# Half a chunk of weights ahead of x, and four pool maps in three products of two parts

## The chip, the core and the metric

The kernel runs on one core of one Trainium2 chip. The metric is the device time of one execution in microseconds (us), the median of several runs. The engines are named as in the profile: PE multiplies matrices (PEld is its loading of stationary operands), DVE and ACT work elementwise on vectors, POOL does the same and indirect transfers, and SP only issues transfers. The queues of SP, ACT and POOL share 16 DMA engines.

## What is computed

A decoder layer on 512 tokens of 1024 features in fp32. A mixing sublayer comes first, then a mixture of 32 experts (top 4), then a gated embedding; each ends in a layer norm. The change lies in the mixing sublayer, and there in the pooling mixer:

```python
proj = x @ w_in[i]                    # (512, 1024) @ (1024, 2048)
v_pool = proj[..., :D_POOL]           # four groups of 128 channels
...
y_pool = pool_mixer(v_pool, pool_mix[i], pool_scale[i])
y_conv = conv_mixer(b_gate, c_gate, v_conv, conv_w[i])
mix = jnp.concatenate([y_pool, y_conv], axis=-1) @ w_out[i]
...
# pool_mixer: group g has the trailing window w = 2, 4, 8, 16
outs.append((cs - lagged) / cnt - vg)                 # the pool difference d
y = jnp.einsum('bsgc,gcd->bsgd', d, pool_mix)         # the map: 128 x 128 for each group
return y.reshape(B, S, D_POOL) * pool_scale
```

## The kernel before

**Two parts.** The large products are made from two parts of each operand: a high part rounded to the format that the listing calls F32R (`nc.scalar.copy`, on ACT), and the low part, the difference (`nc.vector.tensor_sub`, on DVE). `mm3` (line 210) issues three products for each pair of operands: high with low, high with high, low with high. They are lines 213, 214 and 215 in the profile, whatever calls them.

**Weights.** All weights pass through a ring of buffers of 1 MB in chunks, in a fixed order: `load` (line 96) issues the next chunk on SP's queue, `split` (line 105) makes its two parts, `done` gives the buffers back and starts the loads that now have room. The first chunk of the input projection is loaded in two halves of 512 KB, 128 columns each (`c_in[0]`); the other seven hold 256 columns.

**The start.** x comes in four blocks of 128 tokens. SP's queue holds block 0, the first half chunk, block 1, the second half chunk, blocks 2 and 3, and then the other chunks. `turned(i)` transposes block i on PE in two halves of four (line 315, into PSUM tiles `tr`, of which there are two), and for each half ACT writes the high part `xh` (line 394) and DVE the low part `xl` (line 395). `keep_warm` (line 204) issues products whose results nobody reads; `WARM_START` says how many stand before block 0, before block 1 and after it. Then `columns` runs the first half chunks on the first 256 tokens, with blocks 2 and 3 turned between.

**The projection.** The loop at line 486 goes through the chunks in the order 0, 1, 4, 6, 2, 5, 7, 3; a chunk of 256 columns takes 48 products of 512 columns. The program's order is written out by hand, and every engine runs its instructions in that order:

```python
for f in (pool_diff, pool_map):
    for m in pools:
        f(m)
```

Chunks 0 and 1 hold the pool groups (1 and 0, then 3 and 2). After a chunk, `pool_sums` copies its columns out of PSUM and makes the trailing sums on DVE or POOL. One chunk later, behind that chunk's 48 products, `pool_diff` (lines 448 to 451, DVE) makes the difference d, and `pool_map` (line 460) maps it: one product in fp32, 128x512 (line 463; PE runs it as two passes, two records of the profile), a scaled copy on ACT (line 464), and `mixed` (line 454), which writes the two parts of the mixed tokens into the tiles `y`: four casts on ACT (line 457) and four subtractions on DVE (line 458), one for each block of tokens. `y` is read again by the output projection, `project`, after the loop. `bsp` is a tile that `bias_parts` fills during the output projection.

Of the kernel before, what the change touches and what calls it, by code (L numbers as in the profile page):

```python
# [10 lines left out]
F32 = mybir.dt.float32  # L11
F32R = mybir.dt.float32r
# [8 lines left out]
P = 128  # L21
S = 512
NT = S // P
D = 1024
# [12 lines left out]
SPARE = 1  # L37
RING = 14

WARM_START, WARM_ROUTE, WARM_END = (6, 7, 7), (2, 2, 2), (8, 3)  # L40
TURN1 = 5
EMBED = 18
MAXOV = 32
# [5 lines left out]
def tile_layer(ctx: ExitStack, tc: tile.TileContext, x, p, w_in, pool_mix, pool_scale, conv_w, w_out,  # L49
               ln1_g, ln1_b, router_w, router_b, w_gate_up, b_gate_up, w_down, b_down,  # L50
               ln2_g, ln2_b, ple_proj, ple_gate_w, ple_gate_b, ln3_g, ln3_b, out):
    nc = tc.nc
# [8 lines left out]
    def at(name, b, dtype, n=2048, offset=0):  # L61

        return nc.alloc_sbuf_tensor_at(name, [P, n], dtype, offset=base0 + 8192 * b + 4 * offset).ap()
# [6 lines left out]
    def big(n=P):  # L70
        return ps.tile([n, 2, 512], F32, tag="big", name="big", bufs=3)
# [15 lines left out]
    def take(dtype, *kinds):  # L87

        b = next(k for k in kinds if k).popleft()
        return (b[0].tile([P, 2048], dtype, tag=b[1], name="chunk") if type(b) is tuple else ring[b][dtype == F32R]), b  # L90
# [5 lines left out]
    def load(queue=nc.sync, *kinds):  # L96
        j = nloaded[0]
        src, shape = chunks[j]
        t, b = take(F32, *(kinds or (free,)))
        t = t[:, :shape[0] * shape[1]].rearrange("p (a b) -> p a b", a=shape[0])  # L100
        raws[j] = t, b
        queue.dma_start(t, src)
        nloaded[0] += 1
# [26 lines left out]
    def splittable():  # L130
        n, two = room(nsplit[0])
        moved = type(raws[nsplit[0]][1]) is tuple
        return n > moved and two >= moved
# [24 lines left out]
    def splits(n=E):  # L158
        while n and nsplit[0] < min(limit[0], used[0] + lookahead[0]):
            if nloaded[0] == nsplit[0]:  # L160
                load()
            if not splittable():
                break
            split()
            n -= 1
            fill()
# [37 lines left out]
    def keep_warm(n, a, b, o=None):  # L204

        o = big()[:, 0, :b.shape[-1]] if o is None else o
        for _ in range(n):
            nc.tensor.matmul(o, a, b, start=True, stop=True)  # L208

    def mm3(o, ah, al, bh, bl, start, stop, a_late=False):  # L210

        first, last = ((ah, bl), (al, bh)) if a_late else ((al, bh), (ah, bl))
        nc.tensor.matmul(o, *first, start=start, stop=False)  # L213
        nc.tensor.matmul(o, ah, bh, start=False, stop=False)  # L214
        nc.tensor.matmul(o, *last, start=False, stop=stop)  # L215
# [44 lines left out]
    bsp = cp.tile([P, F], F32R, name="bsp")  # L260
# [106 lines left out]

    pro = tc.alloc_tile_pool(name="pro", bufs=1)

    y = [at(f"y{i}", RING + i, F32R) if i < NT - 1 else pro.tile([P, 2 * D], F32R, name="y") for i in range(NT)]  # L370
    y = [[t[:, k * D:(k + 1) * D].rearrange("p (c t) -> p c t", c=ND) for k in range(2)] for t in y]
    with tc.tile_pool(name="mix", bufs=1, side=RIGHT) as q:
        cols16 = q.tile([16, P], F32, name="cols16")
        pmix = q.tile([P, 4, P], F32, name="pmix")
# [3 lines left out]
        xl = q.tile([P, ND, S], F32R, name="xl")  # L378
        with tc.tile_pool(name="xin", bufs=1, side=RIGHT) as xp:
            xs = [xp.tile([P, D], F32, tag="xs", name="xs", bufs=NT) for _ in range(NT)]  # L380
            for i in range(NT):
                nc.sync.dma_start(xs[i], x[0, i * P:(i + 1) * P, :])
                if i < 2:
                    load()
            load()
            nc.sync.dma_start(cols16[:12], conv_w[0].rearrange("k (j p) -> (k j) p", p=P))
            nc.sync.dma_start(cols16[12:16], pool_scale[0].rearrange("(j p) -> j p", p=P))
            nc.sync.dma_start(pmix, pool_mix[0].rearrange("g c d -> c g d"))
            fill()

            def turned(i):
                def put(h, t):
                    o = (slice(None), slice(4 * h, 4 * h + 4), slice(i * P, (i + 1) * P))
                    nc.scalar.copy(xh[o], t)
                    nc.vector.tensor_sub(xl[o], t, xh[o].bitcast(F32))
                transposed(xs[i], P, put)

            def columns(o, cs, b, ts_, between={}):

                wh, wl = (parts[cs[b]] if len(cs) == 2 else (q[:, :, b * P:(b + 1) * P] for q in parts[cs[0]]))  # L400
                for k in range(ND):
                    if k in between:
                        turned(between[k])
                    mm3(o[:, b, ts_], wh[:, k], wl[:, k], xh[:, k, ts_], xl[:, k, ts_], k == 0, k == ND - 1,
                        a_late=True)

            keep_warm(WARM_START[0], ident, ident)
            turned(0)
            splits(1)
            keep_warm(WARM_START[1], ident, ident)  # L410
            turned(1)
            keep_warm(WARM_START[2], ident, ident)
            splits(1)
            o1 = big()
            columns(o1, c_in[0], 0, slice(0, 256), {4: 2})
            columns(o1, c_in[0], 1, slice(0, 256), {2: 3})
            for b in range(2):
                columns(o1, c_in[0], b, slice(256, S))
            splits()
# [2 lines left out]
        cols = q.tile([P, 16], F32, name="cols")  # L422
        nc.vector.tensor_copy(cols, tcol)
        wp = tc.alloc_tile_pool(name="wide", bufs=1, side=RIGHT)

        def wide(tag):
            return wp.tile([P, 16 + S], F32, tag=tag, name=tag, bufs=4)

        held = {}
# [24 lines left out]
        def mixed(c, v):  # L454
            for i, (yh, yl) in enumerate(y):
                ts_ = slice(i * P, (i + 1) * P)
                nc.scalar.copy(yh[:, c], v[:, ts_])
                nc.vector.tensor_sub(yl[:, c], v[:, ts_], yh[:, c].bitcast(F32))

        def pool_map(g):  # L460
            t = tr([P, S])
            d = held.pop(("d", g))
            nc.tensor.matmul(t, pmix[:, g], d, start=True, stop=True)
            nc.scalar.activation(d, t, AF.Copy, scale=cols[:, 12 + g:13 + g])
            mixed(g, d)

# [15 lines left out]
            nc.vector.tensor_mul(v, o, v)  # L482
            mixed(4 + m, v)

        pools = []
        for j, cs in zip(order_in, c_in):
            o = o1 if len(cs) == 2 else big()
            for b in range(2):
                if len(cs) == 1:
                    columns(o, cs, b, slice(0, S))  # L490
            for f in (pool_diff, pool_map):
                for m in pools:
                    f(m)
            pools = []
            for b in (1, 0):
                kind, m = divmod(2 * j + b, 4)
                (pool_sums, conv_out, conv_gate, conv)[kind](m, o[:, b])
                if kind == 0:
                    pools.append(m)
            for c in cs:  # L500
                parts.pop(c)
                done(c)
            splits()
# [401 lines left out]
    for e in range(E):  # L905
# [3 lines left out]
        for o, n, c in halves:  # L909
            r, s = slice(c // 16, c // 16 + 32), slice(e // 16 * 512, e // 16 * 512 + 512)  # L910
            nc.tensor.matmul(o[:, n], sel[r, e % 16:e % 16 + 1].to_broadcast([32, CAP]), bsp[r, s],
                             start=True, stop=False)
# [226 lines left out]
```

## Time and profile before

| | |
|---|---|
| median of 3 runs | 1401.81 us (1401.22 to 1402.82) |
| the profiled execution | 1401.93 us |
| its span, first to last instruction | 1400.1 us |
| mean granted clock of PE | 0.996 |
| PE busy | 1378.5 us, 98% |
| DVE busy | 1225.1 us, 88% |
| ACT busy | 948.1 us, 68% |
| POOL busy | 480.8 us, 34% |
| read from memory | 443.97 MB, 331 GB/s over the span |

An engine's busy time counts its own work, not its waits. A record of a product lasts longer than the pace at which products follow one another, because they are pipelined; costs on PE are therefore read from the starts of records. A line of a timeline gives start, duration, engine, line of the program, operation, written tile and read tiles, shapes, how many records are merged, and in brackets the idle time before the first of them and what ended it. Line numbers are those of the kernel before.

### The profile page before, as it was taken

The page shows a single profiled execution, that of the slowest core. Times are in us where ns is not written, and L with a number is a line of the kernel's source. Part 1 is how long each engine was busy: PE and PEld are TensorE (multiplying, and loading weights), DVE is VectorE, ACT ScalarE, POOL GpSimd, SP SyncE. Part 2 cuts the span into 40 slices and gives each one's busy share as a digit, 9 for nine tenths or more (in the row PEclk, how much of TensorE's full clock was granted, in tenths as well). Part 3 has the DMA queues.
Part 4 walks back from the last instruction along what each step waited for, and adds up shares of the span by engine and source line. Part 5 has one row for each costly group of instructions (what it writes and reads, how often), then busy time and mean ns, then how long its engine had stood idle before and what let it go on. Part 6 is the DMA issues. An engine that isn't in the chain of part 4 may idle for free. (4 is left out here: it accounts for less than half of the span.)

```text
span 1400.1 us, 17688 instructions
## 1 busy us (share of the span) xinstructions
PE 1378.5 (98%) x6605; PEld 987.5 (71%) x6605; DVE 1225.1 (88%) x1078; ACT 948.1 (68%) x740; POOL 480.8 (34%) x171
## 2 busy tenths in 40 slices
PE   9999999999999999999999999999999999999996
PEld 8788767766677777676777667666666666666675
DVE  6645599999999999999989999999999999999875
ACT  5321267777777777777777778777777777777631
POOL 1101114533333333333333363545454545442100
PEclk9999999999999999999999999999999999999999
DMA  9327889999999999999989999999999999999511
GB/s 330 129 90 241 331 315 367 370 376 386 375 380 380 378 369 385 384 374 381 323 318 335 376 381 396 371 394 391 385 357 386 381 385 367 365 388 363 172 47 46
DMA packets 98264, 464.44 MB, mean 332 GB/s; under 512 B 9488, under 2 KB 19232, under 8 KB 65408
## 3 DMA queue, kind: packets, MB, share of 16 engines
q1 hardware_dynamic: 86640, 427.85, 78.9%
q0 software_dynamic: 9536, 33.44, 9.6%
q10 hardware_dynamic: 2000, 1.98, 0.5%
q8 instruction: 54, 0.88, 0.3%
q14 instruction: 34, 0.28, 0.1%
HBM read 443.97 MB, written 19.27 MB: 331 GB/s over the span
## 5 line engine op out<-in xcount | busy, mean ns | idle before, releaser
L321 POOL DMA_INDIRECT xg<-x1d,idxg x31 | 227.9, 7350 | 254.9 <-ACT chunk L114 109.4
L361 POOL DMA_INDIRECT acc<-yo,idxs x32 | 179.7, 5615 | 39.3 <-ACT yo L360 23.8
L213 PE MATMUL big<-chunk,xl 128*96 128x512 f32 x480 | 190.3, 396 | 0.0
L214 PE MATMUL big<-chunk,xh 128*96 128x512 f32 x480 | 189.0, 394 | 0.0
L346 POOL TENSOR_SCALAR h<-h 96x1024 f32<-96x1024 f32 x32 | 41.0, 1280 | 401.5 <-ACT h L345 401.5
L213 PE MATMUL big<-chunk,hl 128*96 128x512 f32 x268 | 106.4, 397 | 0.0
L214 PE MATMUL big<-chunk,hh 128*96 128x512 f32 x268 | 104.9, 391 | 0.0
L213 PEld LDWEIGHTS big<-chunk,xl 128*96 128x96 f32 x480 | 77.4, 161 | 34.9 <-issue 3.4
L214 PEld LDWEIGHTS big<-chunk,xh 128*96 128x96 f32 x480 | 77.4, 161 | 30.8
L214 PEld LDWEIGHTS big<-chunk,hh 128*96 128x96 f32 x268 | 43.7, 163 | 17.5
L213 PEld LDWEIGHTS big<-chunk,hl 128*96 128x96 f32 x268 | 43.1, 161 | 17.1
L349 ACT ACTIVATE sg<-gm 96x1024 f32<-96x1024 f32 x32 | 34.0, 1064 | 16.2 <-DVE gm L343 16.2
L330 ACT CAST xh<-tr 128x384 fp32r<-128x384 f32 x64 | 27.4, 480 | 25.4 <-PE tr L315 25.4
L360 ACT ACTIVATE yo<-big,gs 96x1024 f32<-96x1024 f32 x31 | 34.4, 1111 | 13.4 <-PE big L215 13.4
L299 POOL TENSOR_TENSOR mv<-mv,mhalf 128x1 f32<-128x1 f32 x12 | 7.8, 653 | 97.2 <-DVE mv L298 97.2
L330 ACT CAST hh<-tr 128x384 fp32r<-128x384 f32 x62 | 26.5, 479 | 20.3 <-PE tr L315 20.3
L353 DVE SCALAR_TENSOR_TENSOR h<-h,gm 96x1024 f32<-96x1024 f32 x32 | 38.9, 1215 | 0.2
L351 DVE TENSOR_TENSOR gm<-gm,sg 96x1024 f32<-96x1024 f32 x32 | 38.9, 1215 | 0.1
L343 DVE TENSOR_SCALAR gm<-big 96x1024 f32<-96x1024 f32 x32 | 38.7, 1210 | 0.0
L117 DVE TENSOR_TENSOR ring12dt.float32r<-ring12dt.float,ring6dt.float32r 128x2048 fp32r<-128x2048 f32 x14 | 32.0, 2287 | 4.9 <-ACT ring6dt.float32r L114 4.9
L345 ACT COPY h<-big 96x1024 f32<-96x1024 f32 x32 | 32.6, 1020 | 5.4 <-PE big L215 5.4
L117 DVE TENSOR_TENSOR ring9dt.float32r<-ring9dt.float,ring2dt.float32r 128x2048 fp32r<-128x2048 f32 x14 | 32.0, 2288 | 4.0 <-ACT ring2dt.float32r L114 4.0
(583 smaller groups left out, 4397.6 us busy)
## 6 DMA issues: line engine op xcount, KB each, us to landing
ring13dt.float<-in_w_gate_up_dram SPq DMA_DIRECT2D x18, 1024.0 KB, 9.2
ring10dt.float<-in_w_gate_up_dram SPq DMA_DIRECT2D x18, 1024.0 KB, 7.8
ring1dt.float<-in_w_gate_up_dram SPq DMA_DIRECT2D x18, 1024.0 KB, 8.5
ring2dt.float<-in_w_gate_up_dram SPq DMA_DIRECT2D x18, 1024.0 KB, 8.4
ring3dt.float<-in_w_gate_up_dram SPq DMA_DIRECT2D x18, 1024.0 KB, 8.5
ring4dt.float<-in_w_gate_up_dram SPq DMA_DIRECT2D x18, 1024.0 KB, 9.5
ring9dt.float<-in_w_gate_up_dram SPq DMA_DIRECT2D x17, 1024.0 KB, 9.2
ring5dt.float<-in_w_gate_up_dram SPq DMA_DIRECT2D x17, 1024.0 KB, 7.3
```

The lines of the kernel that those rows point to most:

```text
L117: second()
L213: nc.tensor.matmul(o, *first, start=start, stop=False)
L214: nc.tensor.matmul(o, ah, bh, start=False, stop=False)
L321: nc.gpsimd.indirect_dma_start(out=xg, out_offset=None, in_=x1d, in_offset=bass.IndirectOffsetOnAxis(ap=idxg[:, e:e + 1], axis=0))
L330: nc.scalar.copy(hi[:, 4 * h:4 * h + 4], t)
L343: nc.vector.tensor_scalar(gm, gp, LIMIT, None, op0=ALU.min)
L346: nc.gpsimd.tensor_scalar(h, h, LIMIT, -LIMIT, op0=ALU.min, op1=ALU.max)
L349: nc.scalar.activation(sg, gm, AF.Sigmoid, scale=SW_ALPHA)
L351: nc.vector.tensor_mul(gm, gm, sg)
L353: nc.vector.scalar_tensor_tensor(h, h, 1.0, gm, op0=ALU.add, op1=ALU.mult)
L360: nc.scalar.activation(y, o.rearrange("p a b -> p (a b)"), AF.Copy, scale=gate)
L361: nc.gpsimd.indirect_dma_start(out=acc, out_offset=bass.IndirectOffsetOnAxis(ap=idx, axis=0), in_=y, in_offset=None, compute_op=ALU.add)
```

## The change

The first half chunk of weights is loaded ahead of x, and the second behind block 1. At the start the split of the first half chunk is issued ahead of block 0, that of the second right behind block 1, and the warm-up calls are 13, 2 and 3. The map weights `pmix` are split into two parts `mh` and `ml`, which lie in `bsp`. Behind the chunk in which `pool_map` stood, `pool_parts` now writes the two parts of d to the places in `y` where the group's mixed tokens will stand; one chunk later `pool_map` makes the map from the parts with `mm3`, in 384 columns (the three blocks that now lie in one tile, `y012`) and 128 (the last block), and `mixed` overwrites the places.

```diff
--- before.py
+++ after.py
@@ -37,7 +37,7 @@
 SPARE = 1
 RING = 14
 
-WARM_START, WARM_ROUTE, WARM_END = (6, 7, 7), (2, 2, 2), (8, 3)
+WARM_START, WARM_ROUTE, WARM_END = (13, 2, 3), (2, 2, 2), (8, 3)
 TURN1 = 5
 EMBED = 18
 MAXOV = 32
@@ -367,7 +367,8 @@
 
     pro = tc.alloc_tile_pool(name="pro", bufs=1)
 
-    y = [at(f"y{i}", RING + i, F32R) if i < NT - 1 else pro.tile([P, 2 * D], F32R, name="y") for i in range(NT)]
+    y012 = at("y012", RING, F32R, (NT - 1) * 2048).rearrange("p (i q) -> p i q", i=NT - 1)
+    y = [y012[:, i] if i < NT - 1 else pro.tile([P, 2 * D], F32R, name="y") for i in range(NT)]
     y = [[t[:, k * D:(k + 1) * D].rearrange("p (c t) -> p c t", c=ND) for k in range(2)] for t in y]
     with tc.tile_pool(name="mix", bufs=1, side=RIGHT) as q:
         cols16 = q.tile([16, P], F32, name="cols16")
@@ -378,9 +379,10 @@
         xl = q.tile([P, ND, S], F32R, name="xl")
         with tc.tile_pool(name="xin", bufs=1, side=RIGHT) as xp:
             xs = [xp.tile([P, D], F32, tag="xs", name="xs", bufs=NT) for _ in range(NT)]
+            load()
             for i in range(NT):
                 nc.sync.dma_start(xs[i], x[0, i * P:(i + 1) * P, :])
-                if i < 2:
+                if i == 1:
                     load()
             load()
             nc.sync.dma_start(cols16[:12], conv_w[0].rearrange("k (j p) -> (k j) p", p=P))
@@ -404,13 +406,13 @@
                     mm3(o[:, b, ts_], wh[:, k], wl[:, k], xh[:, k, ts_], xl[:, k, ts_], k == 0, k == ND - 1,
                         a_late=True)
 
+            splits(1)
             keep_warm(WARM_START[0], ident, ident)
             turned(0)
-            splits(1)
             keep_warm(WARM_START[1], ident, ident)
             turned(1)
+            splits(1)
             keep_warm(WARM_START[2], ident, ident)
-            splits(1)
             o1 = big()
             columns(o1, c_in[0], 0, slice(0, 256), {4: 2})
             columns(o1, c_in[0], 1, slice(0, 256), {2: 3})
@@ -423,6 +425,10 @@
         nc.vector.tensor_copy(cols, tcol)
         wp = tc.alloc_tile_pool(name="wide", bufs=1, side=RIGHT)
 
+        mh, ml = (bsp[:, k * 512:(k + 1) * 512].rearrange("p (g d) -> p g d", g=4) for k in range(2))
+        nc.scalar.copy(mh, pmix)
+        nc.vector.tensor_sub(ml, pmix, mh.bitcast(F32))
+
         def wide(tag):
             return wp.tile([P, 16 + S], F32, tag=tag, name=tag, bufs=4)
 
@@ -457,10 +463,17 @@
                 nc.scalar.copy(yh[:, c], v[:, ts_])
                 nc.vector.tensor_sub(yl[:, c], v[:, ts_], yh[:, c].bitcast(F32))
 
+        def pool_parts(g):
+
+            mixed(g, held["d", g])
+
         def pool_map(g):
             t = tr([P, S])
             d = held.pop(("d", g))
-            nc.tensor.matmul(t, pmix[:, g], d, start=True, stop=True)
+
+            dh, dl = (y012[:, :, k * D + g * P:k * D + (g + 1) * P] for k in range(2))
+            mm3(t[:, :S - P].rearrange("p (i t) -> p i t", t=P), mh[:, g], ml[:, g], dh, dl, True, True)
+            mm3(t[:, S - P:], mh[:, g], ml[:, g], y[-1][0][:, g], y[-1][1][:, g], True, True)
             nc.scalar.activation(d, t, AF.Copy, scale=cols[:, 12 + g:13 + g])
             mixed(g, d)
 
@@ -482,16 +495,18 @@
             nc.vector.tensor_mul(v, o, v)
             mixed(4 + m, v)
 
-        pools = []
+        pools, ready = [], []
         for j, cs in zip(order_in, c_in):
             o = o1 if len(cs) == 2 else big()
             for b in range(2):
                 if len(cs) == 1:
                     columns(o, cs, b, slice(0, S))
-            for f in (pool_diff, pool_map):
+            for m in ready:
+                pool_map(m)
+            for f in (pool_diff, pool_parts):
                 for m in pools:
                     f(m)
-            pools = []
+            pools, ready = [], pools
             for b in (1, 0):
                 kind, m = divmod(2 * j + b, 4)
                 (pool_sums, conv_out, conv_gate, conv)[kind](m, o[:, b])
```

PE at the start of the program (`big<-ident` are the warm-up calls, `tr<-ident,xs` the transposes of a block, `big<-xl` and `big<-xh` the first products of the projection):

```order
-L208 MATMUL big<-ident 128x128 x6
+L208 MATMUL big<-ident 128x128 x13
 L315 MATMUL tr<-ident,xs 128x128 x8
-L208 MATMUL big<-ident 128x128 x7
+L208 MATMUL big<-ident 128x128 x2
 L315 MATMUL tr<-ident,xs 128x128 x8
-L208 MATMUL big<-ident 128x128 x7
+L208 MATMUL big<-ident 128x128 x3
 L213 MATMUL big<-xl,ring9dt.float32r 128x256
```

Most of the warm-up calls now stand ahead of block 0, and three are left between block 1 and the first product.

ACT in the same place (`xh<-tr` are the high parts of x, `ring9dt` and `ring10dt` those of the two half chunks); DVE has the low parts in the same order:

```order
-L394 CAST xh<-tr 128x4x128 x2
 L114 CAST ring9dt.float32r<-ring0dt.float_63 128x1024
-L394 CAST xh<-tr 128x4x128 x2
+L396 CAST xh<-tr 128x4x128 x4
 L114 CAST ring10dt.float32r<-ring1dt.float_65 128x1024
-L394 CAST xh<-tr 128x4x128 x4
+L396 CAST xh<-tr 128x4x128 x4
 L114 CAST ring11dt.float32r<-ring2dt.float_67 128x2048
```

The first half chunk's part moved ahead of block 0, and blocks 0 and 1 now follow one another.

PE behind the third chunk of the projection (`ring12dt` and `ring3dt` are that chunk's parts; `tr<-v,pmix` are maps as before, `tr<-y,bsp` maps from parts):

```order
 L215 MATMUL big<-xh,ring3dt.float32r 128x512
-L463 MATMUL tr<-v,pmix 128x512 x2
+L213 MATMUL tr<-y_160,bsp 128x384
+L214 MATMUL tr<-y_160,bsp 128x384
+L215 MATMUL tr<-y_160,bsp 128x384
+L213 MATMUL tr<-y,bsp 128x128
+L214 MATMUL tr<-y,bsp 128x128
+L215 MATMUL tr<-y,bsp 128x128
```

Where the maps of groups 3 and 2 stood, the maps of groups 1 and 0 now stand, the second of them in six products like these; the maps of groups 3 and 2 follow behind the fourth chunk.

## Rows read from the trace of the kernel before

**Rows 1.** The page, busy time of the engines.

```profile
PE 1378.5 (98%) x6605; PEld 987.5 (71%) x6605; DVE 1225.1 (88%) x1078; ACT 948.1 (68%) x740; POOL 480.8 (34%) x171
```

**Rows 2.** Busy time by stretch: us, engines busy (instructions), PEclk, DMA share, GB/s.

```profile
35.00:110.00 75.00, 74.47 (x312) 58.22 (x313) 40.97 (x70) 23.60 (x48) 8.03 (x15) 1.00 0.32 113
...
170.00:1000.00 830.00, 827.64 (x3952) 577.93 (x3953) 776.76 (x601) 627.83 (x448) 331.24 (x80) 1.00 0.98 370
```

**Rows 3.** Waits of the matmul engine, whole span: total us, times, longest.

```profile
PE tr L648 <- DVE xl L331: 0.8, 1, 0.8
PE tr L315 <- DMA xs<-in_x_dram: 0.7, 2, 0.5
```

**Rows 4.** Timeline of PE, 1 to 10.6 us: start, us, engine, line, operation, tiles.

```profile
1.38 2.93 PE L208 MATMUL big<-ident 128*128 128x128 f32 x12 [1.38 <-DVE ident L225]
4.54 1.09 PE L315 MATMUL tr<-ident,xs 128*128 128x128 f32 x8 [0.22 <-DMA xs<-in_x_dram]
...
7.72 1.07 PE L315 MATMUL tr<-ident,xs 128*128 128x128 f32 x8 [0.52 <-DMA xs<-in_x_dram]
...
10.10 0.36 PE L213 MATMUL big<-xl,ring9dt.float32r 128*128 128x256 f32 x1
```

**Rows 5.** Warm-up products by form, 0 to 4.4 and 5.4 to 7.3 us: busy, mean ns.

```profile
L208 PE MATMUL big<-ident 128*128 128x128 f32 x12 | 2.9, 434 | 1.4 <-DVE ident L225 1.4
...
L208 PE MATMUL big<-ident 128*128 128x128 f32 x14 | 1.7, 275 | 0.0
```

**Rows 6.** Timeline of the SP queue, then DMA issues (KB each, us from issue to landing).

```profile
1.17 0.42 SPq L102 DMA_DIRECT2D ring0dt.float<-in_w_in_dram  x1
...
ring0dt.float<-in_w_in_dram SPq DMA_DIRECT2D x1, 512.0 KB, 5.0
```

**Rows 7.** Timelines of ACT and DVE, 5 to 13 us.

```profile
6.24 1.06 ACT L114 CAST ring9dt.float32r<-ring0dt.float 128x1024 fp32r<-128x1024 f32 x1
...
5.90 1.29 DVE L395 TENSOR_TENSOR xl<-tr,xh 128x512 fp32r<-128x512 f32 x2 [2.51 <-ACT xh L394]
7.33 1.22 DVE L117 TENSOR_TENSOR ring0dt.float32r<-ring0dt.float,ring9dt.float32r 128x1024 fp32r<-128x1024 f32 x1
9.00 1.29 DVE L395 TENSOR_TENSOR xl<-tr,xh 128x512 fp32r<-128x512 f32 x2 [0.45 <-ACT xh L394]
```

**Rows 8.** Timeline of PE around the four maps.

```profile
33.30 0.39 PE L213 MATMUL big<-xl,ring11dt.float32r 128*128 128x512 f32 x1
...
34.47 0.40 PE L215 MATMUL big<-xh,ring2dt.float32r 128*128 128x512 f32 x1
35.20 2.00 PE L463 MATMUL tr<-v,pmix 128*128 128x512 f32 x4 [0.34 <-issue]
...
37.27 0.39 PE L214 MATMUL big<-xh,ring12dt.float32r 128*128 128x512 f32 x1
...
48.01 0.40 PE L215 MATMUL big<-xh,ring3dt.float32r 128*128 128x512 f32 x1
48.73 1.97 PE L463 MATMUL tr<-v,pmix 128*128 128x512 f32 x4 [0.33 <-DVE v L451]
...
50.77 0.40 PE L214 MATMUL big<-xh,ring13dt.float32r 128*128 128x512 f32 x1
```

**Rows 9.** Timeline of PE, products of 256 columns; eight more lie between these.

```profile
10.42 0.28 PE L215 MATMUL big<-xh,ring0dt.float32r 128*128 128x256 f32 x1
...
11.47 0.28 PE L215 MATMUL big<-xh,ring0dt.float32r 128*128 128x256 f32 x1
```

**Rows 10.** Timeline of DVE, 34 to 50 us.

```profile
34.94 0.16 DVE L451 TENSOR_TENSOR v<-s,v 128x3 f32<-128x3 f32 x1
...
38.91 0.90 DVE L458 TENSOR_TENSOR y<-v,y 128x128 fp32r<-128x128 f32 x4 [0.62 <-ACT y L457]
...
46.78 1.51 DVE L448 SCALAR_TENSOR_TENSOR v<-s,v 128x497 f32<-128x497 f32 x1
...
49.29 0.17 DVE L451 TENSOR_TENSOR v<-s,v 128x7 f32<-128x7 f32 x1
```

## The prediction, made before the change was run

> **What bounds the kernel now.** I read the page first, then the stretches, then the waits, then the timelines of the first 50 us. The matrix engine (PE) is busy 98% of the span [rows 1], and in the two long stretches, the input projection from 35 to 110 us and the experts from 170 to 1000 us, it is busy 74.5 of 75.0 and 827.6 of 830.0 us [rows 2]. Its waits are few: the only row that names a transfer is the arrival of x at the very start, 0.7 us in two waits, and the longest wait inside the expert stage is 0.8 us, for DVE [rows 3]. So the end is set by the sum of what PE executes plus its few gaps. A microsecond taken from PE at the start should come off the end, because what follows (expert loads, splits, gathers) is released by PE's own products; a microsecond added to ACT or DVE there costs nothing while they have room: in 35 to 110 us DVE is busy 41 us and ACT 23.6 us of 75 [rows 2]. The change touches only the first 60 us, at two places: the start of the projection, and the four pool maps.
>
> **The start.** Before, x's first block is first in the queue and the first weights second. PE starts on x's first block at 4.54, right on its arrival, and the weights land at 1.17 + 5.0 = 6.17 [rows 4, 6]. Now the weights go first (0.42 us of issue on SP [rows 6]), so block 0 of x takes the second place. Both are 512 KB from one queue, so I take 6.2 for its transposes, 1.65 later. What follows by the old distances: the first half of a turned block leaves its PSUM buffer when DVE has its low part, 5.90 + 0.65 = 6.55, which is 2.0 after PE began, and the second half at 7.19, 2.65 after [rows 4, 7]. There are two such buffers, so block 1, whose x was there at 7.72 [rows 4], can begin at 6.2 + 2.0 = 8.2 instead. From its beginning to DVE's work on its low part it took 9.00 - 7.72 = 1.28 [rows 4, 7], and the half takes 0.65: the first projection product can run at 8.2 + 1.28 + 0.65 = 10.15 or a little over, say 10.2. Before it ran at 10.10 [rows 4], though its data was complete at 9.65: the seven warm-up calls ahead of it kept PE. So the old start was set by filler, the new one by data, and the difference is **+0.1 us**. What was won, that the weights' split (1.06 on ACT, 1.22 on DVE [rows 7]) is no longer between the two blocks, goes into waiting for x. The bounds: -0.4 (it starts when the data was complete before) and +1.05 (rival three).
>
> The warm-up calls move with this: 6, 7, 7 become 13, 2, 3, two records to a call. The first twelve records ran at (2.9 - 0.43)/11 = 0.22 us each, fourteen later ones at (1.7 - 0.275)/13 = 0.11 [rows 5], the ratio of the two clock levels, 1.2 and 2.4 GHz (read off the durations; the granted clock of the page shows no such stretch). Twenty-six records then end near 1.38 + 12 x 0.22 + 14 x 0.11 = 5.6, ahead of 6.2; the four and the six end before the data they lead to. They cost nothing; with x early, those left over would cost 0.11 each.
>
> **The pool maps.** Before, each pair of maps stands behind a chunk's 48 products and needs pool differences that DVE finishes only then: 34.94 + 0.16 = 35.10, and PE's map starts at 35.20 [rows 8, 10]. The products before come every (34.47 - 33.30)/5 = 0.234 us [rows 8]. From the last one before a pair to the second one after it PE took 37.27 - 34.47 = 2.80 and 50.77 - 48.01 = 2.76, where two paces are 0.47 [rows 8]. The pairs cost **2.33 and 2.29, together 4.62 us**; some 0.5 of each is the wait (35.20 against 34.47 + 0.23 = 34.70), the rest, 1.84, four passes of 512 columns at 0.46.
>
> Now a pair is two times three products of 384 columns and three of 128, in the format of the projection. 384 columns by its pace: 0.75 x 0.234 = 0.176. A product of 128 columns in this format stands nowhere in the trace. Lower bound: half of the 256-column pace, (11.47 - 10.42)/9 = 0.117 [rows 9], so 0.058. Upper bound: as the old format, a quarter of two passes of 0.46, so 0.23. I take 0.115: every record here brings its own load of 128 weight columns, and the shortest records that do, the 128-column warm-up passes, follow at 0.11 [rows 5], no faster than the 256-column products with twice the columns. A pair is then 6 x 0.176 + 6 x 0.115 = 1.75, two pairs 3.50: **-1.12 us**; with the bounds 0.058 and 0.23, -1.8 and +0.25. The Trainium skill bears on this against the split into a long and a short piece: "TensorE: Matmul & The Clock Gate", section LDWEIGHTS, says a load's time goes with the weights' columns alone, some 107 ns for 128, so that a short product would not outrun its load; by that figure the pairs would come to 3.40 and the time, as an estimate, to 1400.7. No run here shows it for this format.
>
> Is the wait really gone? The first pair's parts are now cast and subtracted one chunk before PE wants them. DVE's differences are pushed back by the new split of the maps, 128x512, about 0.7, and the parts follow; before, even with the maps in between, they were done at 38.91 + 0.90 = 39.8 [rows 10], and PE wants them at 48.01 + 0.23 [rows 8], less the 2.33 of the pair that is gone, plus 0.1: 46.0: seven us of room. The second pair is tighter, since its differences now queue on DVE behind the first pair's mixing, which waits for PE's maps. That mixing ended 39.8 - 35.2 = 4.6 after the maps began, so 50.6; the differences take 49.46 - 46.78 = 2.7 [rows 10], the parts 1.3 more, since ACT and DVE share them: 54.6. PE wants them at 46.0 + 1.75 + 48 x 0.234 = 59.0. Room of 4.4 us. The extra parts, four groups of four casts and four subtractions (0.90 us a group on DVE [rows 10], on ACT the like), are 3.6 us on each, under idle time. If that cover went, PE would wait at the second pair first.
>
> **Sum.** +0.1 - 1.12 = -1.0 us. The profiled execution took 1401.93 (span 1400.1, 1.8 around it) and becomes 1400.9; it lay 0.1 above the median of 1401.81, so I predict **1400.8**. Differences under 0.2%, 2.8 us, I call no change, and this is one.
>
> **Rivals.**
> One: the short products run at the old format's rate, 0.23. For it: 128 columns are few and nothing in the trace shows this format so narrow. Against it: 256 columns still run at the full pace. The pairs become 4.87, the sum +0.35: 1402.2.
>
> Two: their loads hide wholly, 0.058: the pairs 2.81, the sum -1.7: 1400.1. Against it stand the 0.11 of [rows 5]. The Trainium skill, same page, section on the back-to-back issue gap, has a stream of 128-column products with their loads at some 81 ns; by that the pairs would be 3.08 and the time, as an estimate, 1400.4; the nearest rows here are slower.
>
> Three, slower: the first weights and block 0 of x share the transfer engines and both land at 6.2. ACT and DVE work in order, and the weights' split now stands ahead of block 0, so 1.06 + 1.22 [rows 7] comes first: x's first half has its low part at 9.15 and the projection starts at 9.15 + 1.28 + 0.65 = 11.1, 1.05 late. PE would stand still in between; if the granted clock then fell to 1.2 GHz for as long as at the beginning, twelve records at 0.22 instead of 0.11 show the price, 1.3 to 1.4 more. Sum 1.05 + 1.35 - 1.12 = +1.3: 1403.1, more if the fall lasts. It decides from a landing of the weights after 5.2 (DVE must be through by 7.55). Against it: block 0 of x, first in the queue and as large, was there by 4.54, 1.6 ahead of the second.
>
> Four: the gain doesn't reach the end, because the experts' transfers, busy 98% at 370 GB/s [rows 2], set the pace: 1401.8. Against it: PE is busy 827.6 of 830 there and no wait names a transfer.
>
> **Numbers.** My forecast 0.55, rival one 0.17, two 0.10, three 0.10, four 0.08. Range 1399.0 to 1403.2: from the sum of the lower bounds, -1.8 - 0.4, less the half spread of the runs shown (0.6), up to rival three. Under 1399.0 I put a third of rival two and a tenth of my own case: 0.08. Over 1404.6 half of rival three and a little of one: 0.07. The rest, 0.85, is no measurable change.
>
> **What would show it.** In the new profile: PE's first projection product at 10.2 (over 11: rival three); the six plus six products between two chunks taking 1.75 us, the 128-column ones 0.115 apart (0.23: rival one; 0.06: rival two); no wait of PE on DVE there; PE's first expert product 1 us earlier, and the end too (if only the first: rival four). A gap ahead of the second pair would show my room of 4.4 us wrong, and a gap in the experts that was not there before would make the whole sum wrong.

## The result: 8.4 us slower, and the profile after

| | before | changed |
|---|---|---|
| median | 1400.68 us (6 runs, 1399.79 to 1402.82) | 1409.09 us (6 runs, 1407.48 to 1411.30) |
| profiled execution, its span | 1401.93, 1400.1 | 1408.78, 1407.0 |
| mean granted clock | 0.996 | 0.994 |

The ratio on record is 1.0057, with a 95% interval from 1.0046 to 1.0068 (it is estimated from all the runs and need not be the quotient of the two medians): slower by more than 0.2%, and outside the predicted range. The two profiled executions differ by 6.85 us; the medians differ by 1.6 more, most likely from how executions of one kernel fall (a part on this stands behind the experiments). One of the 20 runs of the kernel before that serve experiment 7 took 3514 us and is left out of the ratios there.

The waits of PE after the change, the first two rows (total us, times, longest), have a transfer at their head, which stood nowhere in [rows 3]:

```profile
PE big L213 <- DMA ring15dt.float<-in_w_gate_up_dram: 5.6, 1, 5.6
PE big L1043 <- issue: 2.2, 1, 2.2
```

The timeline of PE after the change (start, duration, the idle time before in brackets): the start, the first pair of maps, and the output projection from the last product of block 1 to the router's first product (L592, which is L577 before). The blocks are the four blocks of tokens; block 0 is the first, and the third is the one in the third part of `y`.

```profile
1.38 4.62 PE L208 MATMUL big<-ident 128*128 128x128 f32 x26 [1.38 <-DVE ident L225]
6.19 1.09 PE L315 MATMUL tr<-ident,xs 128*128 128x128 f32 x8 [0.20 <-DMA xs<-in_x_dram]
...
8.30 1.25 PE L315 MATMUL tr<-ident,xs 128*128 128x128 f32 x8 [0.57 <-DVE xl L397]
...
10.45 0.36 PE L213 MATMUL big<-xl,ring9dt.float32r 128*128 128x256 f32 x1 [0.23 <-DVE xl L397]
...
46.04 0.40 PE L215 MATMUL big<-xh,ring3dt.float32r 128*128 128x512 f32 x1
46.27 0.34 PE L213 MATMUL tr<-y,bsp 128*128 128x384 f32 x1
...
46.80 0.22 PE L213 MATMUL tr<-y,bsp 128*128 128x128 f32 x1
46.85 0.27 PE L214 MATMUL tr<-y,bsp 128*128 128x128 f32 x1
46.97 0.27 PE L215 MATMUL tr<-y,bsp 128*128 128x128 f32 x1
47.08 0.39 PE L213 MATMUL tr<-y,bsp 128*128 128x384 f32 x1
47.31 0.34 PE L214 MATMUL tr<-y,bsp 128*128 128x384 f32 x1
...
48.23 0.39 PE L214 MATMUL big<-xh,ring13dt.float32r 128*128 128x512 f32 x1
...
127.25 0.39 PE L215 MATMUL big<-ring12dt.float32r,y 128*128 128x512 f32 x1
133.21 0.80 PE L213 MATMUL big<-ring4dt.float32r,y 128*128 128x512 f32 x1 [5.57 <-DMA ring15dt.float<-in_w_gate_up_dram]
133.81 0.63 PE L214 MATMUL big<-ring4dt.float32r,y 128*128 128x512 f32 x1
...
139.80 1.93 PE L592 MATMUL tr<-early,rw 128*32 128x128 f32 x16
```

The same two places in the output projection before, and two in the last 80 us, of which more below (timeline of PE before the change):

```profile
128.10 0.39 PE L215 MATMUL big<-ring12dt.float32r,y 128*128 128x512 f32 x1
128.32 0.39 PE L213 MATMUL big<-ring4dt.float32r,y 128*128 128x512 f32 x1
...
132.72 1.93 PE L577 MATMUL tr<-early,rw 128*32 128x128 f32 x16
...
1324.19 0.73 PE L1028 MATMUL big<-bd,gt 96*128 96x512 f32 x2 [2.37 <-issue]
...
1330.37 0.50 PE L213 MATMUL big<-ring4dt.float32r,p 128*128 128x512 f32 x1 [0.64 <-ACT after L864]
```

The stretches after the change (busy us of PE, PEld, DVE, ACT, POOL; granted clock; DMA share; GB/s):

```profile
120.00:127.00 7.00, 7.00 (x32) 5.82 (x31) 4.57 (x6) 0.00 (x0) 2.37 (x6) 1.00 0.60 160
...
128.00:131.00 3.00, 0.00 (x0) 0.00 (x0) 2.86 (x7) 0.00 (x0) 0.07 (x1) 0.96 1.02 341
131.00:137.00 6.00, 3.79 (x13) 3.30 (x14) 2.49 (x4) 0.98 (x2) 2.02 (x3) 0.50 0.55 221
137.00:140.00 3.00, 3.00 (x13) 2.16 (x13) 0.00 (x0) 0.19 (x1) 0.00 (x0) 0.91 0.22 87
...
170.00:1000.00 830.00, 826.80 (x3976) 578.71 (x3976) 773.64 (x605) 625.14 (x448) 325.93 (x82) 1.00 0.99 370
```

The third block of the output projection should follow the second at 127.25 + 0.23 = 127.48, 0.84 ahead of before: so far the gain is there. It starts at 133.21, **5.73 late**, when a 1 MB load of the first expert's weights into buffer 15 of the ring lands. PE stands still, and the granted clock, 1.00 up to 127, is 0.50 (1.2 GHz) from 131 to 137. From the block's first product to L592 it took 139.80 - 133.21 = 6.59, before 132.72 - 128.32 = 4.40: **2.19 more**. Together 7.92, less 0.84, is 7.08, the shift of L592 (139.80 against 132.72); at the span's end 6.9 of it are left. The experts run as before (826.8 busy us of 830 against 827.6 [rows 2]).

Why should a block that multiplies mixed tokens by output weights wait for an expert's load? The tiles `y` lie where ring buffers 14, 15 and 16 are. Behind `project(1)` the kernel gives buffer 15 back (`more(RING + 1)`), and SP issues the load into it (timeline of SP's queue after the change):

```profile
127.67 0.33 SPq L102 DMA_DIRECT2D ring15dt.float<-in_w_gate_up_dram  x1
```

It lands 5.5 us later. In the kernel before the same load takes 7.5 us, and nothing waits for it: the load has not become slow. `project(2)` reads the third part of `y`, in buffer 16: other bytes. But in the changed kernel the three parts are one tile, `y012`, and that tile overlaps buffer 15. A listing of the changed program's instructions on PE has the wait at this product (in brackets; `y_160` is the joined tile), where the one of the kernel before has none:

```
L215 MATMUL big<-ring12dt.float32r,y_160 128x512
L213 MATMUL big<-ring4dt.float32r,y_160 128x512 [waits DMAHW4_49]
L214 MATMUL big<-ring4dt.float32r,y_160 128x512
```

The wait is thus one that the program itself carries.

**Theory:** between tiles that overlap, the program's waits go by the tile and not by the bytes that are read, so joining the tiles made the wait; the clock's fall follows from it; maps and start are worth about what was predicted. **Rivals:** the load is late because the change moved the traffic; or the 2.2 us are not the clock's; or the gain at the maps comes from their new format, not from their new place.

### The profile page after: what moved, and what is told of

Read it like the earlier page. It is cut to its first block, busy times and chain, and to the rows that moved or that the text cites. A ratio compares the mean times of both kernels' runs of the same rounds, so it can differ in the third digit from the quotient of the medians.

```text
span 1407.0 us, 17756 instructions
## 1 busy us (share of the span) xinstructions
PE 1380.4 (98%) x6617; PEld 991.2 (70%) x6617; DVE 1227.9 (87%) x1095; ACT 951.9 (68%) x757; POOL 477.5 (34%) x171
## 5 line engine op out<-in xcount | busy, mean ns | idle before, releaser
L321 POOL DMA_INDIRECT xg<-x1d,idxg x31 | 222.2, 7168 | 254.9 <-ACT chunk L114 109.3
L361 POOL DMA_INDIRECT acc<-yo,idxs x32 | 182.6, 5707 | 39.3 <-ACT yo L360 24.1
```

The costliest lines, as they stand in the source:

```text
L321: nc.gpsimd.indirect_dma_start(out=xg, out_offset=None, in_=x1d, in_offset=bass.IndirectOffsetOnAxis(ap=idxg[:, e:e + 1], axis=0))
L361: nc.gpsimd.indirect_dma_start(out=acc, out_offset=bass.IndirectOffsetOnAxis(ap=idx, axis=0), in_=y, in_offset=None, compute_op=ALU.add)
```

## The experiments

**1. The joined tile alone** (kernel before, with this and nothing else of the change):

```diff
-    y = [at(f"y{i}", RING + i, F32R) if i < NT - 1 else ...
+    y012 = at("y012", RING, F32R, (NT - 1) * 2048).rearrange(...)
+    y = [y012[:, i] if i < NT - 1 else ...
```

> The kernel before with y0, y1 and y2 as parts of one tile, nothing else. Theory A: the same wait of 5.5 to 5.7 us and the same fall of the clock, with none of the gain: 7.9 us slower than before (span near 1408.0). Rivals B and C: no difference from before, within 0.5 us.

Measured: 1409.41 us (4 runs) against 1400.29, ratio 1.0071, interval 1.0054 to 1.0088. PE's waits have the same first row, without a map or a start having been touched:

```profile
PE big L213 <- DMA ring15dt.float<-in_w_gate_up_dram: 5.7, 1, 5.7
```

And so has the timeline of PE:

```profile
133.75 0.80 PE L213 MATMUL big<-ring4dt.float32r,y 128*128 128x512 f32 x1 [5.71 <-DMA ring15dt.float<-in_w_gate_up_dram]
```

Two lines that compute nothing cost the whole loss: 9.1 us in the medians, 7.5 in the spans of the profiles (1407.6 against 1400.1), where 7.9 was expected.

**2. The load later** (the changed kernel):

```diff
     project(1, {3: [(bias_parts, 0)]})
-    more(RING + 1)
     norm(1)
     project(2, {0: [(turn, 0)], 2: [(route, 0)], 4: [(choose, 0)]})
+    more(RING + 1)
     more(RING + 2)
```

> The whole change with the joined tile, but the buffer ring15 is given back behind the third block of the output projection, together with ring16, so the load into it is issued some 14 us later. Theory A: no wait, as nothing of the joined tile is read behind the load; 0.8 us faster than before if the chunk is still there in time, which its place as the sixth chunk of the first expert suggests. Rival D (the load is needed that early): a new wait on ring15 in the first expert, up to some us.

Measured: 1401.40 (10 runs) against 1400.29, ratio 1.0005 (0.9995 to 1.0014); 7.7 us less than the changed kernel. The load is issued at 141.98, and the third block follows the second without a gap (timeline of PE):

```profile
127.25 0.39 PE L215 MATMUL big<-ring12dt.float32r,y 128*128 128x512 f32 x1
127.48 0.39 PE L213 MATMUL big<-ring4dt.float32r,y 128*128 128x512 f32 x1
...
1323.07 1.22 PE L1043 MATMUL big<-bd,gt 96*128 96x512 f32 x2 [2.30 <-issue]
```

No wait of PE names this load any more, in the first expert either, so rival D falls. The expected 0.8 us under before can't be read from the medians: this one is 1.1 above, and its interval holds 1. The trace has the gain: the third block is 0.84 ahead of before, and the product of `bd` and `gt` near the end 1.1 ahead (1323.07 against 1324.19). So this run holds the whole change without its fault.

**3. Two names for the same bytes** (the changed kernel; the parts go through `y012`, the mixed tokens again through three tiles of their own):

```diff
-    y = [y012[:, i] if i < NT - 1 else ...
+    y = [at(f"y{i}", RING + i, F32R) if i < NT - 1 else ...
+    ypart = [y012[:, i] for i in range(NT - 1)] + y[-1:]
...
-            mixed(g, held["d", g])
+            mixed(g, held["d", g], ypart)
```

> The whole change, but the mixed tokens of blocks 0 to 2 are again written and read through three tiles y0, y1, y2; only the parts of the differences and the maps use the joined tile y012 over the same bytes. Theory A (PE's wait at the third block of the output projection comes from the joined tile alone): the wait of 5.6 us on the transfer into ring15 and the stretch at half clock behind it are gone; what stays is the start 0.35 later and the maps 1.2 cheaper, so 0.8 us faster than before (span near 1399.2). Rival B (the parts lying in the mixed tokens' places make the wait): still 7 us slower. Rival C (the earlier program or the longer mixing makes the transfer late, whatever the tiles): still 5 to 7 us slower.

Measured: 1406.67 (4 runs) against 1400.29, ratio 1.0050 (1.0033 to 1.0066). The wait for the load is gone, as expected: the third block follows the second without a gap (134.37 and 134.60). But my total missed (6.4 above before, not 0.8 under it). That the time is near what rivals B and C gave is chance, since the loss lies elsewhere: two new waits stand at the maps, where I had expected none. The first of PE's waits (L465 is the subtraction of `mixed`, line 458 before):

```profile
PE tr L213 <- DVE y L465: 3.8, 2, 1.9
```

And the first pair in the timeline of PE:

```profile
46.82 0.27 PE L215 MATMUL tr<-y,bsp 128*128 128x128 f32 x1
48.93 0.44 PE L213 MATMUL tr<-y,bsp 128*128 128x384 f32 x1 [1.83 <-DVE y L465]
...
51.27 0.63 PE L215 MATMUL big<-xh,ring4dt.float32r 128*128 128x512 f32 x1
```

The second map of a pair reads its group's columns through `y012`, and the first map's mixed tokens have just been written through `y0` to `y2`: other columns, overlapping tiles. After each wait of 1.9 us the granted clock fell here too (0.50 from 50 to 52, where the record at 51.27 lasts 0.63, not 0.39; and 0.58 from 66 to 68). From the first projection product to the third block it took 134.60 - 10.30 = 124.3 where the run with the later load has 127.48 - 10.48 = 117.0: 3.8 of waits and 3.5 behind them. The miss speaks for the theory: what waits changed with the tile by which the bytes are named. It also narrows it. In the changed kernel, where parts and mixed tokens both go through `y012`, the program has the same writes between the two maps, and the second map still follows the first at once (46.97 and 47.08 in the section on the result). So inside one tile the bytes decided; the waits came where the same bytes have a second name.

**4. The gap filled** (the changed kernel, with 50 warm-up records ahead of the third block):

```diff
     norm(1)
+    keep_warm(25, ident, ident, tr([P, P]))
     project(2, ...
```

> The whole change with 25 warm-up calls (50 records of 0.11 us, 5.6 us) ahead of the third block of the output projection, where PE waits. If the loss is a wait of 5.7 us and 2.2 us of products at half clock behind it: the wait stays, the granted clock stays at 1.00, and the time is 2.2 us below the changed kernel, 4.9 us above before. If the clock's part is smaller or has another reason (transfers, buffers), nothing is gained, or the filler adds to the wait.

Measured: 1407.50 (4 runs) against 1400.29, ratio 1.0058 (1.0041 to 1.0074): 7.2 above before, where 4.9 was expected, and 1.6 less than the changed kernel's median. The timeline of PE:

```profile
127.68 5.75 PE L208 MATMUL tr<-ident 128*128 128x128 f32 x50
135.13 0.50 PE L213 MATMUL big<-ring4dt.float32r,y 128*128 128x512 f32 x1 [1.70 <-DMA ring15dt.float<-in_w_gate_up_dram]
...
139.64 1.93 PE L592 MATMUL tr<-early,rw 128*32 128x128 f32 x16
```

The stretch that had a granted clock of 0.50 now has 1.00:

```profile
131.00:137.00 6.00, 4.30 (x34) 3.93 (x34) 2.69 (x5) 0.44 (x1) 2.10 (x3) 1.00 0.60 230
```

From the block to L592 it is 139.64 - 135.13 = 4.51 at clock 1.00, not 6.59: the 2.1 us are the clock's. At the end this can't be read: here the block starts 7.25 us after the load's issue at 127.88, in the changed kernel 5.54 after 127.67, which took 1.9 back, and L592 is only 0.16 earlier. Whether the filler delayed the load is not shown: the load took 7.5 us in the kernel before, where PE works meanwhile, and 5.6 in run 1, where it stands. The span is 1.7 shorter than the changed kernel's (1405.3 against 1407.0), and 1.6 of it comes from the last 80 us (4.57 there against 6.18; see below), not from the filler.

**5. The maps' place and their format apart.** Kernel before, with the fp32 maps one chunk later and nothing else:

```diff
-            for f in (pool_diff, pool_map):
-                for m in pools:
-                    f(m)
-            pools = []
+            for m in ready:
+                pool_map(m)
+            for m in pools:
+                pool_diff(m)
+            pools, ready = [], pools
```

> The kernel before with its maps in fp32 one chunk later and nothing else: the wait of a half microsecond ahead of each pair goes, the passes stay. If the wait is 0.5 of each pair: pairs of 1.85, third block of the output projection at 127.35, 1.0 earlier. Then the three products of two parts are worth only 0.1 to 0.15 a pair over the passes of fp32. Rival (the format pays, the wait was short): pairs of 2.2, 0.2 to 0.3 earlier in all.

Measured: 1400.55 (10 runs) against 1401.51, ratio 0.9999 (0.9989 to 1.0009). The timeline of PE:

```profile
46.05 0.40 PE L215 MATMUL big<-xh,ring3dt.float32r 128*128 128x512 f32 x1
46.28 1.88 PE L463 MATMUL tr<-v,pmix 128*128 128x512 f32 x4
...
48.23 0.39 PE L214 MATMUL big<-xh,ring13dt.float32r 128*128 128x512 f32 x1
...
127.49 0.39 PE L213 MATMUL big<-ring4dt.float32r,y 128*128 128x512 f32 x1
...
1323.20 0.73 PE L1029 MATMUL big<-bd,gt 96*128 96x512 f32 x2 [2.30 <-issue]
...
1327.76 0.50 PE L213 MATMUL big<-ring4dt.float32r,p 128*128 128x512 f32 x1 [0.64 <-ACT after L865]
```

By the prediction's measure the pair costs 48.23 - 46.05 - 0.47 = **1.71** (1.85 was expected), in the changed kernel 48.23 - 46.04 - 0.47 = **1.72**, before 2.33 and 2.29. At the later place the three products of two parts are worth nothing; what is won is the wait, and the place alone takes it away. The third block comes at 127.49, not 127.35, since the first product came at 10.48 in this execution. The maps of the changed kernel without its faults (two names as in 3, and both maps of a pair ahead of the mixing of either) say the same, with the new start and with the old one:

```diff
+            held["t", g] = t, d
+
+        def pool_mixed(g):
+            t, d = held.pop(("t", g))
             nc.scalar.activation(d, t, AF.Copy, scale=cols[:, 12 + g:13 + g])
             mixed(g, d)
...
-            for m in ready:
-                pool_map(m)
+            for f in (pool_map, pool_mixed):
+                for m in ready:
+                    f(m)
```

> Two views as in the first experiment (the parts through the joined tile, the mixed tokens through three tiles), and both maps of a pair ahead of the mixing of either, so that no product reads the joined tile right behind a write through a single one. Theory A (waits follow tiles that overlap, not bytes): no wait at the second map, none at the third block of the output projection; that block starts on PE at 127.5 against 128.32 before, and the span is 0.8 below the one before (near 1399.2; the clock in the last 80 us can move it by some 2 us either way). Rival B (the places of the parts are at fault): a wait of 1.8 us or more stays at the maps or at the third block.

> The same, but with the start of the kernel before (x ahead of the weights, warm-up calls 6, 7, 7): the maps alone. First product of the projection at 10.10 as before; the pairs take 1.72 instead of 2.33 and 2.29, so the third block of the output projection starts 1.2 us earlier than before, at 127.1. If the new start had been worth something, this is slower than the kernel with both; by the trace of the changed kernel it should be 0.35 faster than that.

Measured: 1400.86 (10 runs; 0.9998, 0.9988 to 1.0007) and 1400.51 (10 runs; 0.9995, 0.9985 to 1.0004). From first projection product to third block, one trace each: 116.99 and 117.00, with the late fp32 maps 117.01, before 118.22. Neither run has a wait at a map or at the third block, so rival B of the first falls.

How much the place is worth depends on the execution, because PE waits only where it comes before DVE's differences. In the run of the start alone (6) PE came to the first pair 1.0 later than before (timeline of PE):

```profile
35.47 0.40 PE L215 MATMUL big<-xh,ring2dt.float32r 128*128 128x512 f32 x1
...
37.65 0.39 PE L214 MATMUL big<-xh,ring12dt.float32r 128*128 128x512 f32 x1
```

This pair, in fp32 and at its old place, cost 37.65 - 35.47 - 0.47 = 1.71: the passes without the wait. In the run of the joined tile alone the first pair cost 1.77 and the second 2.28.

**6. The start alone** (kernel before, with the change's order of loads and splits and its warm-up calls; the diff is that part of the change):

> The kernel before with the new order of loads, splits and warm-up calls at the start, nothing else. First product of the projection at 10.45 against 10.10, everything behind it 0.35 later: third block of the output projection at 128.7, time 0.35 above before, within what can be told from no change. Rival: the start decides more than the first product (later chunks come late): over 1 us.

Measured: 1400.99 (10 runs) against 1401.51, ratio 0.9999 (0.9990 to 1.0009). The timeline of PE:

```profile
1.38 5.68 PE L208 MATMUL big<-ident 128*128 128x128 f32 x26 [1.38 <-DVE ident L225]
6.90 1.04 PE L315 MATMUL tr<-ident,xs 128*128 128x128 f32 x8
...
11.10 0.36 PE L213 MATMUL big<-xl,ring9dt.float32r 128*128 128x256 f32 x1 [0.23 <-DVE xl L396]
```

Here the 26 warm-up records took 5.68, not 4.62: by the length of the records the clock rose later in this execution (the column of the granted clock shows 1.00 from the start in every run), block 0 began at 6.90 and the first product at 11.10. The third block, expected at 128.7, came at 128.73, but that is luck: the start lost 1.0 and not 0.35, and the first pair, which had no wait here, gave 0.6 back. In six profiles with the new start the first product lies between 10.30 and 11.10, in four with the old one and seven calls between 10.10 and 10.48. The new start wins nothing.

**7. What is left to win.** The late fp32 maps, or the maps in parts as in the last run of 5, each with the old start and fewer filler products ahead of the first projection product:

```diff
-WARM_START, WARM_ROUTE, WARM_END = (6, 7, 7), (2, 2, 2), (8, 3)
+WARM_START, WARM_ROUTE, WARM_END = (6, 7, 4), (2, 2, 2), (8, 3)
```

> Before, with the fp32 maps one chunk later (as in the run of the late maps alone) and the third warm-up call count 4 instead of 7. Main theory: the old start was set by filler, as the prediction says: the first projection product starts when DVE has the first half of block 1's low part, 0.3 to 0.45 us earlier than with seven calls (10.03 instead of 10.48 in the timeline of the late maps, if x lands at the same time), and the whole gain stands at the third projection block: from first product to third block 117.0, third block at 127.0 to 127.1 against 128.3 before, so the median 1.2 to 1.6 us under that of before, 1399.0 to 1399.3 if before reads 1400.5, less what the clock in the last 80 us blurs. Rival: something else holds the first product (the weights' split or the queue), so it stays at 10.3 to 10.5 with a gap in front of it, and the third block at 127.4. Second rival: the gain at the third block doesn't reach the end, median within 0.3 of before.

> The maps in three products of two parts, one chunk later, with both maps of a pair ahead of either's mixing and with two sets of tiles over the same bytes, the old start with a third warm-up call count of 4. Main theory (the format is worth nothing, only the chunk's delay is): equal to the run of the late fp32 maps with the same start, third block within 0.15 us of it and medians within 0.5 us of each other. Rival (the format is worth the 0.2 to 1.1 us of the prediction): third block 0.2 to 1.1 us earlier than there, and the median likewise.

Measured against 1401.28 (20 runs): 1400.41 (11 runs; 0.9994, 0.9985 to 1.0004) and 1400.36 (11 runs; 0.9996, 0.9987 to 1.0005). The timeline of PE in the first:

```profile
10.03 0.36 PE L213 MATMUL big<-xl,ring9dt.float32r 128*128 128x256 f32 x1 [0.24 <-DVE xl L395]
...
127.06 0.39 PE L213 MATMUL big<-ring4dt.float32r,y 128*128 128x512 f32 x1
...
1322.80 0.72 PE L1029 MATMUL big<-bd,gt 96*128 96x512 f32 x2 [2.37 <-issue]
...
1328.96 0.50 PE L213 MATMUL big<-ring4dt.float32r,p 128*128 128x512 f32 x1 [0.63 <-ACT after L865]
```

The third block is where the main theory put it (127.0 to 127.1), 1.26 ahead of before, and the gain reaches the end: 1.4 at 1322.80 against 1324.19, and 1.4 in the span (1398.7 against 1400.1). In the second run the first product is at 10.16 and the third block at 127.16, 117.00 again, and the medians are 0.05 apart: no gain from the format, as the main theory said. Both versions beat the changed kernel by 8.7 us. Against the kernel before, the traces show the gain; the medians, 0.9 lower where 1.2 to 1.6 was expected, don't, since their intervals reach past 1.

**Why medians hide a microsecond.** In the last 80 us PE stands 2.2 to 2.4 us ("issue") ahead of the product of `bd` and `gt`. From there to the next row above, the kernel before takes 1330.37 - 1324.19 = 6.18, with a granted clock of 0.66 from 1324 to 1328. In the profile of the late fp32 maps (run 5, the last two rows) the clock of that stretch is 1.00 and it takes 1327.76 - 1323.20 = 4.56, **1.6 less**. All twelve profiles, one of each kernel, fall on one side or the other: 6.0 to 6.2 in eight, 4.56 to 4.58 in four. Executions of one kernel differ in the same way, as the mean granted clock of each shows: of the 31 runs of the kernel before that serve experiments 5 and 6, the 16 at 0.996 took 1401.3 to 1402.1 us, the five at 0.998 1399.7 to 1400.5. The reason was not found, and the difference is more than the maps and the filler are worth together. Sorted by this clock, which was done only after the fact, the runs of experiment 7 do show the gain: at 0.996 the kernel before took 1401.17 to 1402.64 (10 runs), the two versions 1400.23 to 1401.12 (6 runs) and 1400.22 to 1400.71 (7 runs).

## Why the prediction was wrong

**The step that failed** is the sentence "The change touches only the first 60 us, at two places". It has a third: `y012` is a tile of its own kind, and it touches every reader of `y` and every load into its bytes. The prediction followed the new writes to `y` up to the maps, with their room, and never asked what else overlaps the joined tile. The wait of 5.73 us and the 2.19 us at 1.2 GHz behind it are two terms that its sum doesn't have. Run 1 makes them by the joined tile alone, run 2 removes them, and without them the third block lies 0.84 ahead of before, where the sum had 1.0. The list of signs had the right one in general ("a gap ... that was not there before would make the whole sum wrong"), but at the experts, not ahead of them.

**The maps: right in sum, the old pair wrongly split.** Forecast 1.75 a pair and -1.12; the two pairs took 1.72 and, by the rows below (timeline of PE after the change), 1.71, so -1.19.

```profile
58.95 0.39 PE L215 MATMUL big<-xh,ring4dt.float32r 128*128 128x512 f32 x1
...
61.13 0.39 PE L214 MATMUL big<-xh,ring10dt.float32r 128*128 128x512 f32 x1
```

The 128-column products start 0.05, 0.12 and 0.11 us apart, and the product of 384 columns behind them comes 0.05 later than the pace of 0.176, so each costs some 0.11, as taken (0.115); rivals one (0.23) and two (0.058) fall. In the Trainium skill, "TensorE: Matmul & The Clock Gate", the section LDWEIGHTS has a formula by which a load of 128 columns takes some 107 ns; taken as the least pace of a short product, this made an estimate of 3.40 for two pairs. The section on the back-to-back issue gap of the same page has some 81 ns for a product of 128 columns with its load, which made 3.08. The trace has 3.43 and agrees with the first.

But the sentence "some 0.5 of each is the wait ..., the rest, 1.84, four passes" split the old pair wrongly. The passes alone are 1.71 (runs 5 and 6), and the wait with what follows it costs 0.6 where PE meets DVE as in the profile of before. By the prediction's own figures some 1.0 of its gain was the wait and 0.1 to 0.2 the new format; measured, the whole 1.2 is the wait. It never asked what the later place would give with the old maps, which needs no joined tile.

**The room was there.** PE waits for no part at the maps. In the changed kernel DVE had the parts of the first pair at 37.5 and of the second at 54.1, and PE wanted them at 46.3 and 59.2: 8.8 and 5.1 us of room, for the forecast seven and 4.4. (The seven is 46.0 - 39.8 = 6.2 by the prediction's own figures; nothing hangs on it.)

**The start: mis-sized.** Block 0 at 6.19 (forecast 6.2) and block 1 at 8.30 (8.2) came as worked out; the first product came at 10.45, not 10.2, so +0.35 for +0.1. Of this, 0.1 is block 1, and 0.2 is a term that the sum put at nothing: DVE had the half at 9.61 + 0.65 = 10.26, and the product began 0.19 later; in the first version of run 7 this gap is 0.19 as well. That the old start was "set by filler" holds: with three calls less it began at 10.03, on DVE's data. The term "They cost nothing" for the 26 warm-up records depends on when the clock rises: in run 6 they ran on to about 7 and pushed everything back.

**Rivals three and four** didn't occur. The weights' split ended on DVE at 7.20, and block 0 was not held up. What PE lost at 133 us reached the end nearly whole (6.9 of 7.1), and in the experts no wait of PE names a transfer, before or after.

## What to carry to other kernels

When a change joins, renames or re-views a buffer, list everything that reads, writes or is loaded into any byte of it, at any time in the program, above all under another name: here waits followed overlapping tiles, and a product waited 5.7 us for a load into bytes that it doesn't read. When a change moves an operation and reformats it, price the move alone first; here it was the whole gain, and only the new format needed the joined tile. And where executions fall in two groups 1.6 us apart, read a gain of one microsecond from the trace at a fixed point of the program, or compare runs of the same group, and don't go by the medians of all runs.

## What the runs showed that I had not expected

- A wait of PE can be paid more than once: behind 5.6 us of standing still the granted clock was 0.50 from 131 to 137 (2.2 us more), and behind waits of only 1.9 us it fell too (run 3, 3.5 us more for 3.8 of waiting). With the gap filled by products that nobody reads, and 1.7 us of waiting left, it stayed at 1.00 (run 4).
- Behind the standstill of 2.2 to 2.4 us near 1322, the clock fell in some executions and not in others (0.57 to 0.71, or 1.00, from 1324 to 1328 in the versions that stand there at that time), and the same holds for its first rise: 26 warm-up records took from 4.62 to 5.68 us in six profiles. Why one or the other occurs was not settled.
- One map in fp32 (two passes of 512 columns) costs no more than one in the split format (three products of 384 and three of 128 columns): a pair takes 1.71 us in the one and 1.71 to 1.72 in the other.
